# Loading the first block in two parts, alternating transposes and products on TensorE, and holding the first stores behind chunk 19

## Chip, cores and metric

The kernel runs on one core of one Trainium2 chip. The metric is the device time of one execution in microseconds (us). A core's span in the trace is from its first to its last instruction; it is about 1.5 us shorter than the time.

## The reference, cut to what matters

```python
# x: (16, 2048, 256) f32, so 32768 rows of 1 KB; W: (256, 256); A: (256, 16); B: (16, 256)
W_adapted = W + scale * (lora_A @ lora_B)
W_norm = np.sqrt(np.sum(W_adapted ** 2, axis=0, keepdims=True) + 1e-8)
W_final = W_adapted / W_norm * m
y = x.reshape(-1, 256) @ W_final          # 33.55 MB in, 33.55 MB out
```

## The kernel before

Eight blocks of 4096 rows (4 MB) go through five buffers. SyncE issues the loads, ScalarE the stores, each on its own DMA queue. The first five loads are issued at once; load b waits for store b - 5, which empties its buffer. A block has eight chunks of 512 rows; two chunks are a pair. A pair goes through four engines: GpSimd (POOL) casts it to bf16 into `xb`, TensorE (PE) turns it (eight transposes into `xt_ps`), VectorE (DVE) copies that to `xt`, TensorE multiplies by `w_final` into `y_ps` (16 matmuls), and ScalarE (ACT) copies the result into the block's own buffer, from where it is stored.

```python
parts = [(b * CH, CH) for b in range(NBLK - 1)]              # first chunk, chunks
parts += [(NCH - CH, CH // 2), (NCH - CH // 2, CH // 2)]     # last block in halves
...
for n in range(len(parts)):                                  # loads, on SyncE
    b = parts[n][0] // CH
    if b >= XBUFS and parts[n][0] % CH == 0:
        nc.sync.wait_ge(sem(f"store{b - XBUFS}"), 16)
    load_x(n)
...
for p in range(NPR):                                         # casts, on GpSimd
    if p == 0 or part_of[2 * p - 1] != part_of[2 * p]:
        nc.gpsimd.wait_ge(sem(f"load{part_of[2 * p]}"), 16)
    if p >= NXB:
        nc.gpsimd.wait_ge(sem("turned"), p - NXB + 1)
    nc.gpsimd.tensor_copy(out=xb_bufs[p % NXB][:], in_=...)
...
for g in range(NCH):                                         # results and stores, on ScalarE
    nc.scalar.wait_ge(sem("product"), g + 1)
    nc.scalar.copy(out=x_bufs[b % XBUFS][:, c * J : (c + 1) * J, :], in_=y_ps[g % 2][:])
    n = part_of[g]
    if g == NCH - 1 or part_of[g + 1] != n:
        store_y(n)                                           # after a drain
...
nc.tensor.wait_ge(dv, 8)                                     # w_final is ready
...
turned(0)
with nc.Fori(0, NPR // 2, 1, engines=[PE], head_slot={PE: 128}):
    turned(1)
    product(0)
    product(1)
    turned(0)
```

## Time and profile before

| | before |
|---|---|
| time, median of 4 runs | 163.69 us (163.48 to 163.89) |
| span of the profiled execution | 163.2 us |
| bytes, mean rate over the span | 67.41 MB, 413 GB/s |
| busiest compute engine | PE, 65% |

No compute engine is above 65%, and the DMA engines are full in every slice but the first and the last. So I took the bytes to be the bound (e9 below tests it); a change can then win only where the DMA queues are idle or slow. The prediction shows these rows. One more view: the start in order of time (start us, duration us, engine, line, operation, output and inputs, shapes, count, idle time before).

```profile
11.59 0.76 DVE L192 TENSOR_TENSOR wam<-wa,m_all 128x256 f32<-128x256 f32 x2
12.27 1.75 DVE L195 RECIPROCAL rnorm<-norm 128x256 f32<-128x256 f32 x1
13.83 3.92 POOL L165 CAST xb<-x_sb 128x2048 bf16<-128x2048 f32 x2 [12.15 <-DMA x_sb<-in_x_dram]
14.05 3.98 DVE L198 TENSOR_TENSOR w_final<-wam,rnorm 128x256 bf16<-128x256 f32 x2
```

The two multiplications of `wam` take 0.76 us, the two of `w_final`, with inputs of the same shape, 3.98, beside two casts.

### The profile page before, as it was taken

The page shows a single profiled execution, that of the slowest core. Times are in us where ns is not written, and L with a number is a line of the kernel's source. Part 1 is how long each engine was busy: PE and PEld are TensorE (multiplying, and loading weights), DVE is VectorE, ACT ScalarE, POOL GpSimd, SP SyncE. Part 2 cuts the span into 40 slices and gives each one's busy share as a digit, 9 for nine tenths or more (in the row PEclk, how much of TensorE's full clock was granted, in tenths as well). Part 3 has the DMA queues.
Part 4 walks back from the last instruction along what each step waited for, and adds up shares of the span by engine and source line. Part 5 has one row for each costly group of instructions (what it writes and reads, how often), then busy time and mean ns, then how long its engine had stood idle before and what let it go on. Part 6 is the DMA issues. An engine that isn't in the chain of part 4 may idle for free. (4 is left out here: it accounts for less than half of the span.)

```text
span 163.2 us, 1988 instructions
## 1 busy us (share of the span) xinstructions
PE 105.3 (65%) x786; PEld 85.2 (52%) x786; DVE 47.2 (29%) x44; ACT 63.8 (39%) x67; POOL 62.5 (38%) x39
## 2 busy tenths in 40 slices
PE   1270599789789897898981998619988820892000
PEld 0130577677577775776760867418676610771000
DVE  0429452350532514405230325005051400330000
ACT  3010027548366384473754053900738440062000
POOL 1006381753935738268004940069209003900000
PEclk9999999999999999999998589985899996599755
DMA  5998998998999999999999999999999999998991
GB/s 201 402 498 386 426 474 385 482 418 265 466 426 426 442 410 466 426 394 482 418 426 442 420 426 458 402 458 410 446 414 454 414 446 422 450 442 377 442 430 60
DMA packets 2915, 67.41 MB, mean 413 GB/s; under 512 B 465, under 2 KB 482, under 8 KB 610
## 3 DMA queue, kind: packets, MB, share of 16 engines
q1 hardware_dynamic: 1440, 33.82, 49.0%
q10 hardware_dynamic: 1474, 33.59, 47.8%
q14 instruction: 1, 0.01, 0.0%
HBM read 33.85 MB, written 33.55 MB: 413 GB/s over the span
## 5 line engine op out<-in xcount | busy, mean ns | idle before, releaser
L219 ACT COPY x_sb<-y_ps 128x1024 f32<-128x1024 f32 x64 | 61.9, 1014 | 75.8 <-PE y_ps L281 75.8
L165 POOL CAST xb<-x_sb 128x2048 bf16<-128x2048 f32 x32 | 60.0, 1902 | 79.3 <-DMA x_sb<-in_x_dram 56.0
L281 PE MATMUL y_ps<-w_final,xt 128*128 128x256 bf16 x512 | 64.6, 280 | 12.8 <-PEq L256 12.8
L202 DVE COPY xt<-xt_ps 128x1024 f32<-128x1024 f32 x32 | 38.2, 1221 | 88.1 <-PE xt_ps L267 88.0
L281 PEld LDWEIGHTS y_ps<-w_final,xt 128*128 128x128 bf16 x512 | 48.4, 100 | 28.2 <-issue 19.8
L267 PE MATMUL xt_ps<-identity,xb 128*128 128x128 f32 x264 | 39.1, 309 | 23.1 <-PEq L256 23.1
L267 PEld LDWEIGHTS xt_ps<-identity,xb 128*128 128x128 f32 x264 | 34.9, 161 | 25.8 <-issue 25.6
L198 DVE TENSOR_TENSOR w_final<-wam,rnorm 128x256 bf16<-128x256 f32 x2 | 4.0, 2028 | 0.0
L244 PE MATMUL y_ps<-sq,ones 128*128 128x256 f32 x4 | 2.1, 674 | 1.6 <-DVE sq L187 1.6
L233 PE MATMUL y_ps<-identity,a_nat 128*16 128x128 f32 x2 | 0.6, 397 | 3.6 <-DMA a_nat<-in_lora_A_dram 3.6
L212 ACT ACTIVATE norm<-y_ps,eps_col 128x256 f32<-128x256 f32 x1 | 0.5, 473 | 6.1 <-PE y_ps L244 6.1
L244 PEld LDWEIGHTS y_ps<-sq,ones 128*128 128x128 f32 x4 | 1.2, 323 | 2.3 <-DVE sq L187 2.1
L210 ACT ACT_TABLE_LOAD x1 | 1.3, 1283 | 2.4 <-issue 2.4
L233 PEld LDWEIGHTS y_ps<-identity,a_nat 128*16 128x16 f32 x2 | 0.1, 90 | 3.6 <-issue 3.6
L171 POOL MEMSET xb<- 128x2048 bf16 x1 | 1.8, 1805 | 0.3 <-PE xt_ps L267 0.3
L195 DVE RECIPROCAL rnorm<-norm 128x256 f32<-128x256 f32 x1 | 1.7, 1745 | 0.0
L237 PE MATMUL y_ps<-b_bf,aT 16*128 16x256 bf16 x2 | 0.6, 404 | 1.5 <-DVE aT L180 1.5
L189 DVE COPY m_all<-y_ps 128x256 f32<-128x256 f32 x1 | 0.4, 425 | 3.3 <-PE y_ps L249 3.3
L178 DVE CAST b_bf<-b_nat 16x256 bf16<-16x256 f32 x1 | 0.3, 281 | 3.8 <-DMA b_nat<-in_lora_B_dram 3.8
L249 PE MATMUL y_ps<-m_row,ones 1*128 1x256 f32 x2 | 1.2, 710 | 0.0
L237 PEld LDWEIGHTS y_ps<-b_bf,aT 16*128 16x128 bf16 x2 | 0.1, 106 | 1.9 <-DVE aT L180 1.9
L183 DVE SCALAR_TENSOR_TENSOR wa<-y_ps,w_nat 128x512 f32<-128x512 f32 x1 | 0.7, 692 | 0.8 <-PE y_ps L237 0.8
(13 smaller groups left out, 3.7 us busy)
## 6 DMA issues: line engine op xcount, KB each, us to landing
x_sb<-in_x_dram SPq DMA_DIRECT2D x7, 4096.0 KB, 27.1
out_dram<-x_sb ACTq DMA_DIRECT2D x7, 4096.0 KB, 37.2
x_sb<-in_x_dram SPq DMA_DIRECT2D x2, 2048.0 KB, 29.6
out_dram<-x_sb ACTq DMA_DIRECT2D x2, 2048.0 KB, 20.2
w_nat<-in_W_dram SPq DMA_DIRECT2D x1, 256.0 KB, 2.9
a_nat<-in_lora_A_dram ACTq DMA_DIRECT2D x1, 16.0 KB, 2.6
b_nat<-in_lora_B_dram ACTq DMA_DIRECT2D x1, 16.0 KB, 3.6
m_row<-in_m_dram ACTq DMA_DIRECT2D x1, 1.0 KB
```

What stands on the lines that cost most here:

```text
L165: nc.gpsimd.tensor_copy(out=xb_bufs[p % NXB][:], in_=x_bufs[b % XBUFS][:, 2 * c * J : 2 * (c + 1) * J, :],).then_inc(sem("rounded"), 1)
L171: nc.gpsimd.memset(xb_bufs[NPR % NXB][:], 0.0).then_inc(sem("rounded"), 1)
L183: nc.vector.scalar_tensor_tensor(out=wa[:], in0=ab_ps, scalar=float(scale), in1=w_nat[:], op0=ALU.mult, op1=ALU.add).then_inc(dv, 1)
L195: nc.vector.reciprocal(out=rnorm[:], in_=norm[:]).then_inc(dv, 1)
L198: i = nc.vector.tensor_mul(out=w_final[:, t], in0=wam[:, t], in1=rnorm[:])
L202: nc.vector.tensor_copy(out=xt_bufs[p % NXT][:].rearrange("p r t -> p (r t)").bitcast(FP32), in_=xt_ps[p % 2][:],).then_inc(sem("copied"), 1)
L210: nc.scalar.activation(out=warm[:], in_=eps_col[:], func=AF.Sqrt)
L219: nc.scalar.copy(out=x_bufs[b % XBUFS][:, c * J : (c + 1) * J, :], in_=y_ps[g % 2][:]).then_inc(sem("room"), 1)
L244: i = nc.tensor.matmul(n2_ps, ones[:], sq[:, t, :], start=(t == 0), stop=(t == KC - 1))
L249: nc.tensor.matmul(mb_ps, ones[0:1, :], m_row[:], start=True, stop=True).then_inc(pe, 1)
L267: i = nc.tensor.transpose(xt_ps[p % 2][:, j * P : (j + 1) * P], xb_bufs[p % NXB][:, j, :].bitcast(FP32), identity[:],)
L281: i = nc.tensor.matmul(y_ps[h][:, j, :], xt_bufs[p % NXT][:, r : r + P, t], w_final[:, t, :], start=(t == 0 and (j % (J // 2)) == 0), stop ...
```

## The change

Its intent: start TensorE earlier (the first pair needs only 1 MB, not 4), run it without gaps, and use the time so won to keep the stores back until the five free loads are nearly in, so that reads run alone first. Twelve tiny loads behind the last load mark in the trace when each of the DMA engines has done its loads. In the code, `turned(k)` is the eight transposes of the pair in buffer k and `product(k)` its 16 matmuls. The first cast also waits until VectorE has the squares of the weights (`dve`, 4). The diff, cut to its core (declarations, the DRAM layout of block 0 and the renaming of `parts` are left out):

```diff
+    HOLD = 19
+    MARKS = [1, 2, 3, 4, 5, 6, 8, 10, 12, 14, 15, 16]
-    parts = [(b * CH, CH) for b in range(NBLK - 1)]
-    parts += [(NCH - CH, CH // 2), (NCH - CH // 2, CH // 2)]
+    loads = [(0, 2), (2, CH - 2)] + [(b * CH, CH) for b in range(1, NBLK - 1)]
+    loads += [(NCH - CH, CH // 2), (NCH - CH // 2, CH // 2)]
+    stores = [(b * CH, CH) for b in range(NBLK - 1)]
+    stores += [(NCH - CH, CH // 2), (NCH - CH // 2, CH // 2)]
+    issue = [max(g0 + cnt - 1, HOLD + n) for n, (g0, cnt) in enumerate(stores)]
 ...
+    for q, n in enumerate(MARKS):
+        nc.sync.dma_start(
+            out=marks[0:n, q, 0 : 2 + n], in_=lora_B[0:n, 0 : 2 + n]
+        ).then_inc(sem("marks"), 16)
+    nc.sync.wait_ge(sem("marks"), 16 * len(MARKS))
 ...
+        if p == 0:
+            nc.gpsimd.wait_ge(sem("dve"), 4)
 ...
-        if g == NCH - 1 or part_of[g + 1] != n:
-            ...
-            store_y(n)
+        for n in range(len(stores)):
+            if issue[n] == g:
+                ...
+                store_y(n)
 ...
-    nc.tensor.wait_ge(dv, 8)
-    nc.tensor.sem_inc(sem("room"), 2)
     turned(0)
+    nc.tensor.wait_ge(dv, 8)
+    nc.tensor.sem_inc(sem("room"), 2)
     with nc.Fori(0, NPR // 2, 1, engines=[PE], head_slot={PE: 128}):
         turned(1)
         product(0)
+        turned(0)
         product(1)
-        turned(0)
```

More of the change, by code (lines that the diff above doesn't have):

```diff
@@ L85 @@
     m_all = sb("m_all", [P, OUT], FP32)
+    marks = sb("marks", [16, len(MARKS), 18], FP32)
     w_final = sb("w_final", [P, KC, OUT], BF16)
@@ L103, in sem @@
         return sems[name]
-    parts = [(b * CH, CH) for b in range(NBLK - 1)]
-    parts += [(NCH - CH, CH // 2), (NCH - CH // 2, CH // 2)]
-    part_of = {}
-    for n, (g0, cnt) in enumerate(parts):
-        for g in range(g0, g0 + cnt):
-            part_of[g] = n
+    loads = [(0, 2), (2, CH - 2)] + [(b * CH, CH) for b in range(1, NBLK - 1)]
+    loads += [(NCH - CH, CH // 2), (NCH - CH // 2, CH // 2)]
+    load_of = {g: n for n, (g0, cnt) in enumerate(loads) for g in range(g0, g0 + cnt)}
+    stores = [(b * CH, CH) for b in range(NBLK - 1)]
+    stores += [(NCH - CH, CH // 2), (NCH - CH // 2, CH // 2)]
+    issue = [max(g0 + cnt - 1, HOLD + n) for n, (g0, cnt) in enumerate(stores)]
     def in_sbuf(g0, cnt):
@@ L119, in in_dram @@
     def in_dram(dram, g0, cnt):
+        if g0 + cnt <= CH:
+            block = dram[0:BLK].rearrange("(p j) k -> p j k", p=P)
+            return block[:, g0 * J : (g0 + cnt) * J, :]
         return dram[g0 * J * P : (g0 + cnt) * J * P].rearrange("(p j) k -> p j k", p=P)
@@ L123, in load_x @@
         nc.sync.dma_start(
-            out=in_sbuf(*parts[n]), in_=in_dram(x_flat, *parts[n])
+            out=in_sbuf(*loads[n]), in_=in_dram(x_flat, *loads[n])
         ).then_inc(sem(f"load{n}"), 16)
@@ L128, in store_y @@
         nc.scalar.dma_start(
-            out=in_dram(out_flat, *parts[n]), in_=in_sbuf(*parts[n])
+            out=in_dram(out_flat, *stores[n]), in_=in_sbuf(*stores[n])
         ).then_inc(sem(f"store{n}"), 16)
@@ L140 @@
     nc.scalar.dma_start(out=m_row[:], in_=m[None, :]).then_inc(sem("load_m"), 16)
-    for n in range(len(parts)):
-        b = parts[n][0] // CH
-        if b >= XBUFS and parts[n][0] % CH == 0:
+    for n in range(len(loads)):
+        b = loads[n][0] // CH
+        if b >= XBUFS and loads[n][0] % CH == 0:
             nc.sync.wait_ge(sem(f"store{b - XBUFS}"), 16)
         load_x(n)
+    for q, n in enumerate(MARKS):
[3 more added lines that the diff above has]
+    nc.sync.wait_ge(sem("marks"), 16 * len(MARKS))
     nc.gpsimd.memset(zeros[:], 0.0).then_inc(sem("pool"), 1)
@@ L160 @@
         b, c = divmod(p, PRB)
-        if p == 0 or part_of[2 * p - 1] != part_of[2 * p]:
-            nc.gpsimd.wait_ge(sem(f"load{part_of[2 * p]}"), 16)
+        if p == 0 or load_of[2 * p - 1] != load_of[2 * p]:
+            nc.gpsimd.wait_ge(sem(f"load{load_of[2 * p]}"), 16)
+        if p == 0:
+            nc.gpsimd.wait_ge(sem("dve"), 4)
         if p >= NXB:
@@ L221 @@
         ).then_inc(sem("room"), 1)
-        n = part_of[g]
-        if g == NCH - 1 or part_of[g + 1] != n:
-            nc.scalar.drain().then_inc(sem("done"), 1)
-            nc.scalar.wait_ge(sem("done"), n + 1)
-            store_y(n)
+        for n in range(len(stores)):
+            if issue[n] == g:
+                nc.scalar.drain().then_inc(sem("done"), 1)
+                nc.scalar.wait_ge(sem("done"), n + 1)
+                store_y(n)
     pe = sem("pe")
```

## The prediction

> **What bounds the kernel now.** I read the span and the slice rows of the page first, then its queue rows, then a table of busy time by stretches of my own choosing, and last ScalarE in order of time. The first lines say how much was moved and that it was moved without a pause:
>
> ```profile
> span 163.2 us, 1988 instructions
> PE 105.3 (65%) x786; PEld 85.2 (52%) x786; DVE 47.2 (29%) x44; ACT 63.8 (39%) x67; POOL 62.5 (38%) x39
> ...
> DMA  5998998998999999999999999999999999998991
> ...
> DMA packets 2915, 67.41 MB, mean 413 GB/s; under 512 B 465, under 2 KB 482, under 8 KB 610
> ## 3 DMA queue, kind: packets, MB, share of 16 engines
> q1 hardware_dynamic: 1440, 33.82, 49.0%
> q10 hardware_dynamic: 1474, 33.59, 47.8%
> ```
>
> No compute engine passes 65%. The DMA engines are full in every slice but the first and the last; q1 carries the loads and q10 the stores. The table by stretches shows where the rate is not at its best (columns: stretch, its length, busy us of PE, PEld, DVE, ACT, POOL, clock, DMA share, GB/s; bytes are counted where a packet starts):
>
> ```profile
> 36.00:40.00 4.00, 3.68 (x34) 3.00 (x33) 0.63 (x1) 2.83 (x3) 2.04 (x2) 1.00 1.12 344
> 40.00:136.00 96.00, 73.21 (x576) 60.02 (x574) 28.55 (x24) 47.48 (x50) 41.09 (x22) 0.93 1.00 433
> 136.00:156.00 20.00, 8.33 (x56) 7.06 (x56) 2.45 (x2) 3.85 (x4) 5.54 (x3) 0.76 0.98 423
> 156.00:160.00 4.00, 0.00 (x0) 0.00 (x0) 0.00 (x0) 0.00 (x0) 0.00 (x0) 0.50 0.90 385
> 160.00:163.20 3.20, 0.00 (x0) 0.00 (x0) 0.00 (x0) 0.00 (x0) 0.00 (x0) 0.50 0.05 20
> ```
>
> With the bytes of each packet spread over its duration (my own sum over the packet records), the rate is 432 GB/s from 4 to 36 us, when there are only loads, 432 from 40 to 136, when loads and stores mix, and 432 from 136 to 156, when there are only stores. A 32 KB packet takes 1.213 us in both queues. So a mix of reads and writes costs no rate here. The one hole is 36 to 40 us at 299 GB/s. The first store is issued at 34.5, and from 36.1 on two load packets on each DMA engine take up to 2.9 us; each engine loses about 1.2 us, once.
>
> The end of a store shows another loss. Of the 16 completions of the last store, 15 come between 159.8 and 160.7 us, one at 163.2. One DMA engine lags 2.4 us. It has no lag when the loads alone end at 33.2; its store packets take some 50 ns longer than the 1.213 us from 47.7 to 150.4 us.
>
> This gives a ledger of the span: 2.75 us until packets flow, 67.41 MB at 432 GB/s = 156.0, hole 1.2, lag 2.4, last receipt 0.5. The sum is 162.9 against 163.2. Compute has no term in it. The chain of waits agrees: it stops at 145 us and holds 2% of the span, because from 148 us only stores run.
>
> **What the Trainium skill says.** "DMA: Bandwidth & Descriptors", section "Where 436 GB/s comes from", gives 435 GB/s as the ceiling of the 16 ports and says that HBM, at about 358, binds for transfers between HBM and SBUF. The trace agrees with the first (432) and not with the second. The same page, "Issuing engines are not separate DMA queues", says that transfers from several issuing engines share the same 16 DMA engines: 4 MB loads land 9.70 us apart alone (13.8, 23.5, 33.2) and 19.4 apart in the mix (48.8, 68.1). "SBUF — State Buffer", "Who interferes with whom", says that a VectorE instruction with two SBUF inputs contends with a GpSimd instruction that reads SBUF, and that the second to issue is blocked. The trace agrees: each half of w_final takes 2.03 us beside two casts, each half of wam, with the same inputs, 0.38 without one.
>
> **The change part by part.**
>
> *Block 0 in two loads.* No bytes are added. A 16 KB packet takes 0.611 us, half of a 32 KB one, so cutting 32 KB rows into 8 and 24 KB costs nothing that I can size. The first 1 MB should land near 6 us; the rest still lands at 13.8.
>
> *First turn early, w_final.* The first cast waits for the squares, done at 7.82, and runs 7.9 to 9.8, where VectorE is idle until 11.13. TensorE ends its preamble at 11.1 and turns pair 0 there. The second cast still waits for 13.8, and the third may follow at once, since pair 0 has been turned; so two casts still lie beside reciprocal and w_final, and w_final still ends at 18.0. What is saved is one turn at the slow start: 16 took 3.65 us, so 8 take about 1.8. The first product starts near 20.1 instead of 21.82.
>
> *By turns.* Before, one round of two pairs looks like this on ScalarE:
>
> ```profile
> 30.26 1.93 ACT L219 COPY x_sb<-y_ps 128x1024 f32<-128x1024 f32 x2 [2.45 <-PE y_ps L281]
> 32.49 1.93 ACT L219 COPY x_sb<-y_ps 128x1024 f32<-128x1024 f32 x2 [0.30 <-PE y_ps L281]
> 34.52 0.37 ACTq L128 DMA_DIRECT2D out_dram<-x_sb  x1
> 36.87 1.93 ACT L219 COPY x_sb<-y_ps 128x1024 f32<-128x1024 f32 x2 [2.46 <-PE y_ps L281]
> ```
>
> From 30.26 to 36.87 is 6.61 us for two pairs, 3.31 each. On TensorE that is 16 turns in 1.91, a gap of 0.69 (VectorE has only just begun to copy), 1.91 for a product, a gap of 0.32 (ScalarE has not given y_ps back) and 1.95. By turns, the copy of a pair runs beside the product of the pair before, and ScalarE's copies run beside the next turn, so both gaps go: 0.95 + 1.95 = 2.9 us per pair. POOL at 1.87 and ScalarE at 2.0 per pair fit in that. This saves 0.4 us per pair of compute, 13 us in 32 pairs, all of it beside full DMA queues: worth nothing by itself.
>
> *Stores held.* Product 0 ends near 20.1 + 2.7 = 22.8, product 9 at 22.8 + 9 x 2.9 = 48.9, chunk 19 is copied at 50.0, and store 0 is issued there, not at 34.5; store 1 at 52, store 2 near 56. Until then the loads run alone: block 4 lands at 13.8 + 4 x 9.70 = 52.6. A store starts to act 1.5 us after its issue (34.5 to 36.1), so at 51.5, some 0.6 us before the last load packets end at 52.1. The hole of 1.2 us moves there; as the loads run out in it, it may show as idle engines instead of slow packets. Then stores 0 and 1 run alone. Store 0 needs 9.7 us from about 53.3, lands near 63.8, and only then is load 5 issued (before: at 60.6). From 65.5 the two queues share. Store 1 has 3.1 MB left, 14.4 us in the mix, and load 5 lands near 85 (before 87.7), load 6 near 105 (107.4), the last half of load 7 near 124 (137.2). After that only stores run, some 15.7 MB = 36.3 us: 160, plus lag and receipt, 163. Since load 7 lands earlier by 13 us, and the product is faster, the last store is issued near 134, with about 26 us of stores ahead. The tail stays bound by DMA.
>
> *Marks.* Twelve loads of 12 to 1,152 bytes, issued behind load 7. A packet of 128 bytes takes 13 ns and a completion 9, so the DMA engine that serves all twelve spends about 0.3 us on them (an estimate from these two). If that is the lagging one, the end moves by 0.3.
>
> **Sum.** Bytes and rate: 0. Start: 0. Hole: 0, or up to +2 if chunk 19 comes later than 50.6. Restart of the loads after an empty queue near 65: 0, or a second hole of 1.2, taken at one in four, +0.3. Marks +0.1. Lag: the mix shrinks from about 100 us to 60, but the number of store packets in the slow time hardly changes, so 0 to -0.7. I choose +0.1 us: 163.8 us.
>
> **The rivals.** *Reads alone, then writes alone, are more efficient.* For it: the lag is nil at 33.2 us and grows during the mix, and the hole opens when stores start. If all the lag went, 2.4 us would be won: 161.3. Against it: 432 GB/s in all three kinds of stretch, and the long store packets go on from 137 to 150 us with no load about. *The queue runs dry between the last free load and the first store.* For it: the margin above is half a microsecond, and before, the first store packet starts 5.1 us after the issue. If those 5.1 us are pure latency, the engines idle from 52.1 to 55.1, 3.0 us in place of 1.2; each microsecond by which chunk 19 is late adds one. That gives 165.5 to 167. Against it: in those 5.1 us the load packets themselves are slow, so it looks more like a stall than like latency. *The faster, earlier compute shortens the kernel*: at 13 us of saved product time this would be 150 us. Against it: nothing waits for compute at the end; the last store waits 15.0 us from issue to landing, of which its own 2 MB need 4.9.
>
> **Range and chances.** Two percent are 3.3 us. A gain of 3.3 is more than lag and tail receipt together, so it would take two losses that vanish at once: 4%. A loss of 3.3 us needs the dry queue at its worst: 6%. The range is 161.8 (most of the lag won) to 166.2 (a dry queue of some 2.5 us).
>
> **What would show it.** Right: store 0 issued at 49 to 51 us; about 2.9 us per pair before; a stretch of reads alone at 432 GB/s to 52, one of stores alone to 65; last load landed near 124; the same mean GB/s, with the losses near 52 instead of 36; span 162 to 165. Wrong: a slice near 52 with the DMA share under a half (dry queue), or all 16 completions of the last store within a microsecond (the lag belongs to the mix), or a last store issued after 150 us.

## The result, and the profile after

| | before | after |
|---|---|---|
| time, median of 4 runs | 163.69 us | 163.74 us (163.58 to 163.99) |
| ratio of fast runs | | 1.0005, 95% interval 0.9986 to 1.0024 |
| span of the profiled execution | 163.2 us | 162.2 us |
| store 0 issued | 34.5 us | 45.5 us |
| last load landed | 137.2 us | 136.5 us |
| last store issued | 148.2 us | 149.8 us |

A ratio here and below is the mean time of one kernel's fast runs over that of the other's of the same rounds, so it is not quite the ratio of the medians quoted. Executions over 1.5% slower than the fastest of the same kernel are left out of the means.

The time is the same. The profiled span is 1.0 us shorter, but that is not the change. The profiled execution of before took 164.71 us, longer than any of its four timed runs; in 11 later runs of that kernel, beside the first experiments, the span was 161.9 to 162.7 us. The trace of before is an unusually slow execution, so differences under a microsecond between the two traces mean nothing.

The page of the changed kernel:

```profile
span 162.2 us, 2003 instructions
PE 100.9 (62%) x786; PEld 87.8 (54%) x786; DVE 44.9 (28%) x44; ACT 64.2 (40%) x67; POOL 62.5 (39%) x39
...
DMA  4999999999998999999999999999999999999993
...
DMA packets 3251, 67.42 MB, mean 416 GB/s; under 512 B 673, under 2 KB 690, under 8 KB 818
## 3 DMA queue, kind: packets, MB, share of 16 engines
q1 hardware_dynamic: 1776, 33.82, 49.2%
q10 hardware_dynamic: 1474, 33.59, 48.2%
```

The bytes are the same, and the DMA row is as full. The table by stretches (columns as in the prediction's) shows the losses moved:

```profile
48.00:52.00 4.00, 3.90 (x37) 3.36 (x35) 2.24 (x2) 3.06 (x4) 3.01 (x2) 1.00 1.06 369
52.00:65.00 13.00, 11.61 (x107) 10.62 (x105) 4.90 (x4) 8.65 (x10) 8.06 (x5) 1.00 1.00 431
65.00:136.00 71.00, 37.06 (x283) 32.28 (x281) 14.70 (x12) 23.86 (x25) 18.77 (x10) 0.76 1.00 430
136.00:156.00 20.00, 10.01 (x72) 8.64 (x72) 2.45 (x2) 5.88 (x6) 5.54 (x3) 0.76 1.00 426
156.00:160.00 4.00, 0.00 (x0) 0.00 (x0) 0.00 (x0) 0.00 (x0) 0.00 (x0) 0.50 0.88 377
```

The slow stretch is now at 48 to 52 us, where store 0 joins the loads, instead of 36 to 40. With the bytes spread over the packets' durations, the rate is 432 to 434 GB/s from 6 to 44 us (reads alone), 432 from 56 to 64 (stores alone: the free loads are in, and load 5 waits for store 0, which lands at 63.7), and about 432 in the mix after that. What falls short of 432 GB/s adds up to 0.90 us between 40 and 65 us, against 1.17 us between 5 and 40 us before.

The compute did get faster. ScalarE in order of time:

```profile
27.70 1.93 ACT L237 COPY x_sb<-y_ps 128x1024 f32<-128x1024 f32 x2 [0.72 <-PE y_ps L295]
30.32 1.93 ACT L237 COPY x_sb<-y_ps 128x1024 f32<-128x1024 f32 x2 [0.69 <-PE y_ps L295]
...
45.46 0.37 ACTq L136 DMA_DIRECT2D out_dram<-x_sb  x1
...
149.83 0.34 ACTq L136 DMA_DIRECT2D out_dram<-x_sb  x1
```

A pair takes 30.32 - 27.70 = 2.62 us instead of 3.31. The start also differs:

```profile
7.26 1.89 POOL L183 CAST xb<-x_sb 128x2048 bf16<-128x2048 f32 x1 [5.58 <-DVE sq L205]
...
13.35 0.76 DVE L216 TENSOR_TENSOR w_final<-wam,rnorm 128x256 bf16<-128x256 f32 x2
13.97 3.73 POOL L183 CAST xb<-x_sb 128x2048 bf16<-128x2048 f32 x2 [4.83 <-DMA x_sb<-in_x_dram]
...
17.74 2.91 PE L295 MATMUL y_ps<-w_final,xt 128*128 128x256 bf16 x16
```

Here `w_final` began before the casts and was not held up: 0.76 us instead of 3.98. The first product starts at 17.74 us, not 21.82.

### The profile page after: what moved, and what is told of

It reads as the page before. It is cut to its first block, busy times and chain, and to the rows that moved or that the text cites. A ratio compares the mean times of both kernels' runs of the same rounds, so it can differ in the third digit from the quotient of the medians.

```text
span 162.2 us, 2003 instructions
## 1 busy us (share of the span) xinstructions
PE 100.9 (62%) x786; PEld 87.8 (54%) x786; DVE 44.9 (28%) x44; ACT 64.2 (40%) x67; POOL 62.5 (39%) x39
## 5 line engine op out<-in xcount | busy, mean ns | idle before, releaser
L183 POOL CAST xb<-x_sb 128x2048 bf16<-128x2048 f32 x32 | 60.0, 1893 | 78.6 <-DMA x_sb<-in_x_dram 63.5
L295 PE MATMUL y_ps<-w_final,xt 128*128 128x256 bf16 x512 | 66.8, 288 | 0.1
L220 DVE COPY xt<-xt_ps 128x1024 f32<-128x1024 f32 x32 | 39.2, 1225 | 92.3 <-PE xt_ps L281 92.3
L281 PEld LDWEIGHTS xt_ps<-identity,xb 128*128 128x128 f32 x264 | 33.8, 156 | 44.4 <-issue 44.0
L295 PEld LDWEIGHTS y_ps<-w_final,xt 128*128 128x128 bf16 x512 | 53.0, 104 | 8.4 <-issue 0.4
L267 PEld LDWEIGHTS y_ps<-m_row,ones 1*128 1x128 f32 x2 | 0.5, 308 | 0.7 <-issue 0.7
```

The lines of the kernel that those rows point to most:

```text
L183: nc.gpsimd.tensor_copy(out=xb_bufs[p % NXB][:], in_=x_bufs[b % XBUFS][:, 2 * c * J : 2 * (c + 1) * J, :],).then_inc(sem("rounded"), 1)
L220: nc.vector.tensor_copy(out=xt_bufs[p % NXT][:].rearrange("p r t -> p (r t)").bitcast(FP32), in_=xt_ps[p % 2][:],).then_inc(sem("copied"), 1)
L267: nc.tensor.matmul(mb_ps, ones[0:1, :], m_row[:], start=True, stop=True).then_inc(pe, 1)
L281: i = nc.tensor.transpose(xt_ps[p % 2][:, j * P : (j + 1) * P], xb_bufs[p % NXB][:, j, :].bitcast(FP32), identity[:],)
L295: i = nc.tensor.matmul(y_ps[h][:, j, :], xt_bufs[p % NXT][:, r : r + P, t], w_final[:, t, :], start=(t == 0 and (j % (J // 2)) == 0), stop ...
```

## The experiments

Ten kernels ran. Theory: the bytes at 432 GB/s set the time, and none of the change's parts touches them. Its main rival: a part wins what another loses. "Lost" below is the time by which the rate, with the bytes spread over the packets' durations, falls short of 432 GB/s in a stretch; a recount from the packet records gave the same within 0.2 us.

### e1: without the marks

```diff
-    for q, n in enumerate(MARKS):
-        nc.sync.dma_start(...).then_inc(sem("marks"), 16)
-    nc.sync.wait_ge(sem("marks"), 16 * len(MARKS))
```

> The changed kernel without its twelve marks. Theory (the DMA engines bound both kernels and the marks are a few hundred nanoseconds of work on one of them): 163.6 us, 0 to 0.3 us below the changed kernel. Rival (a small transfer stalls its DMA engine until its receipt is back, so the marks cost a microsecond that the rest of the change had won): 162.6 us or less.

163.61 us, ratio to before 0.9995 (0.9972 to 1.0018). The marks cost nothing that shows.

### e2: without the hold

```diff
-    HOLD = 19
+    HOLD = 0
```

> The changed kernel with its stores issued as soon as a block is done; block 0 in two loads and the turns stay. Theory (faster compute and held stores are both worth nothing, since the rate is 432 GB/s whatever the mix): 163.7 us, store 0 issued near 30 us, the hole of about 1 us right after it. Rival (the hold wins what the rest loses, or the reverse): over 0.5 us away from 163.7.

163.97 us, ratio 1.0011 (0.9990 to 1.0032), with one of six runs slow at 170.09, which is left out. Store 0 was issued at 29.5 us, and 1.0 us was lost right after it, at 31 to 37, as expected. Not expected was the end. Without the hold the stores take their share of the rate earlier, so the loads come later: the last landed at 142.1 us instead of 136.5, and the last two stores were issued at 150.1 and 155.4. Store 6 had largely drained by 150.7, so the queues had little to do:

```profile
148.00:152.00 4.00, 4.00 (x38) 3.68 (x36) 1.23 (x1) 3.12 (x4) 0.00 (x0) 0.97 0.83 349
```

The new order on TensorE has a share in this. `turned(0)` of the next pair now stands before `product(1)` of a block's last pair, and it needs the next load. So the last pair of the first half of block 7, whose load had landed at 127.3, was copied only after the second half had landed at 142.1 (ScalarE, the line with 11.95 us of waiting):

```profile
133.97 1.93 ACT L237 COPY x_sb<-y_ps 128x1024 f32<-128x1024 f32 x2 [0.69 <-PE y_ps L295]
147.85 2.17 ACT L237 COPY x_sb<-y_ps 128x1024 f32<-128x1024 f32 x2 [11.95 <-PE y_ps L295]
150.12 0.34 ACTq L136 DMA_DIRECT2D out_dram<-x_sb  x1
```

The store of that half was issued 22.8 us after its load landed, here and in the changed kernel (121.8 to 144.6), against 10.6 us before (122.3 to 132.9). From 65 to 160 us 1.3 us were lost. Yet the time hardly moved, because the other loss shrank: the 16 completions of the last store fell within 0.7 us, against 2.6 in the changed kernel. The completions of store 6, before the dry stretch, were 2.3 us apart, those of the next store 1.2: it looks as if the lagging DMA engines caught up while the others had nothing to do. So the hold is worth nothing in time here; it moves spare time to the tail.

### e3: store 0 held until chunk 23

```diff
-    HOLD = 19
+    HOLD = 23
```

> The changed kernel with store 0 held until chunk 23, issued near 50.9 us, where the free loads end at about 52.1. Theory (the hole at the first store is a stall of about 1 us, which begins 1.5 us after the issue): no packets for about 1.5 us in all near 53, so 163.7 to 164.5 us. Rival (the 4.5 us from the first issue to the first store packet are pure latency, hidden only while loads remain): engines idle from 52.1 to 55.4, some 3.3 us in place of 0.9, so 166 us.

165.31 us, ratio 1.0094 (1.0074 to 1.0115): between the two expectations, and the trace refutes both. Store 0 was issued at 51.0 us, and its first packet started at 51.87, 0.9 us later, so the 4.5 us of the changed kernel are no fixed latency; only 0.5 us was lost between 40 and 65. Nor is the hole a stall that belongs to the first store, since 1.2 us were now lost later, in two stretches:

```profile
50.00:54.00 4.00, 4.00 (x39) 3.62 (x36) 1.90 (x2) 2.22 (x3) 2.48 (x3) 1.00 1.00 377
66.00:70.00 4.00, 2.97 (x28) 2.51 (x25) 1.22 (x1) 3.31 (x4) 0.00 (x0) 1.00 1.03 377
76.00:80.00 4.00, 0.00 (x0) 0.00 (x0) 0.00 (x0) 0.00 (x0) 0.00 (x0) 0.50 0.91 336
```

At 66 to 70 us load 5 joins the stores, and it is the store packets that are slow. The second stretch, near the end of store 1, has no join to explain it. The runs do not settle the mechanism. What they show is that a queue which joins a full one often costs about a microsecond, and not always: in the changed kernel load 5 joined the stores at 65 us at no cost.

### e4: the hold alone, on the kernel before

```diff
+    issue = [max(g0 + cnt - 1, 19 + n) for n, (g0, cnt) in enumerate(parts)]
-        if g == NCH - 1 or part_of[g + 1] != n:
+        for n in range(len(parts)):
+            if issue[n] == g:
```

> The kernel before with the held stores alone (no early first turn, TensorE in its old order, block 0 in one load, no marks). At 3.31 us per pair chunk 19 is ready at 54.4 us, after the free loads end at 52.1. Theory: the DMA engines idle from 52.1 to about 56.5 or 57.5, 4.4 to 5.4 us, less the 1.2 us of the hole that goes: 166.9 to 168.2 us. Rival (reads alone and then writes alone pay back): 165 us or less.

166.82 us, ratio 1.0182 (1.0158 to 1.0207), just below what was expected: slower, though not surely by 2%. With the old pace store 0 was issued at 54.7 us, after the free loads had landed at 52.6:

```profile
52.00:56.00 4.00, 3.31 (x31) 2.86 (x30) 1.56 (x2) 2.27 (x3) 1.47 (x1) 1.00 0.31 131
...
68.00:72.00 4.00, 3.05 (x27) 2.40 (x25) 2.36 (x2) 1.55 (x3) 3.60 (x2) 1.00 0.90 270
```

The queues were dry for most of 52 to 56 us; 3.8 us were lost there, and 1.6 more when load 5 joined and at 82. This is the one part that was seen to cost time by itself (the early first turn and the new order ran only together, in e2). With the faster compute the cost is gone, since store 0 comes at 45.5 us.

### e5: no compute

The casts, turns, copies and products are taken out, and the blocks are stored as they were loaded. Its output is wrong, which doesn't matter for the time.

```diff
-    for g in range(NCH): ...            # results and stores
+    nc.scalar.wait_ge(sem(f"load{load_of[4 * CH - 1]}"), 16)
+    for n, (g0, cnt) in enumerate(stores):
+        for k in sorted({load_of[g] for g in range(g0, g0 + cnt)}):
+            nc.scalar.wait_ge(sem(f"load{k}"), 16)
+        store_y(n)
```

> The changed kernel without its stages of casts, turns, copies and products; the blocks go out as they came in (wrong on purpose), store 0 behind the load of block 3, which lands at 42.8 us, so near the issue of 45.5. Theory (67.4 MB at 432 GB/s set the time and 100 us of TensorE work set none of it): 162.5 to 163.8 us. If the lag of one DMA engine comes from the compute beside it, the 16 completions of the last store fall within 0.8 us and the time is at the low end. Rival (compute has a share in the end): under 161.5 us.

162.35 us, ratio 0.9925 (0.9891 to 0.9959), a little below what was expected. The page:

```profile
span 161.1 us, 141 instructions
PE 4.4 (3%) x10; PEld 1.9 (1%) x10; DVE 5.8 (4%) x12; ACT 2.0 (1%) x3; POOL 0.7 (0%) x6
...
DMA  4999999999999999999999999999999999999996
```

With 96 us of TensorE work gone, 1.3 us are won. About 1.0 of them lies in the span and shows at the end of the last store; the rest lies outside the span (time less span is 1.3 us here, about 1.5 before). The 16 completions of the last store fall within 1.2 us (3.3 in the trace of before, 2.6 in the changed kernel). Store packets that take 20 to 150 ns too long are 4, against 40 and 38. In this trace no DMA engine lags as before. That the lag comes from the compute is likely, but not shown: this is one trace, another of the four runs took 163.38 us (span 162.1), as long as with compute, and the stores were issued at other times too (the first four at 43.0 to 44.4 us, the last at 135.9). Nor does the number of long packets settle it: e2 has about 145 of them with completions 0.7 us apart, e4 about 90 with 2.0.

### e6: the last block in one load

```diff
-    loads += [(NCH - CH, CH // 2), (NCH - CH // 2, CH // 2)]
+    loads += [(NCH - CH, CH)]
```

(The DRAM side of the last block follows the block's layout, as it does for block 0.)

> The changed kernel with the last block loaded in one transfer of 32 KB rows instead of two of 16 KB rows. Theory (the two queues take turns packet by packet, so 16 KB packets against 32 KB packets get one third of the rate, 140 against 290 GB/s in the trace): load 7 gets 216 GB/s and lands near 127 us instead of 136.5, the last store is issued near 141 instead of 149.8, and the time stays at 163.7, within 0.3, since the last store only waits longer. Rival (the last load is on the path to the end): 161 to 163 us.

Load 7 landed at 126.5 us instead of 136.5. While it ran, both queues moved packets of 32 KB in nearly equal numbers (114 and 110 ended from 109 to 126 us, 220 and 212 GB/s). In the changed kernel, from 109 to 128 us, 168 load packets of 16 KB ended beside 166 store packets of 32 KB, 145 beside 286 GB/s. The queues take turns packet by packet, and the smaller packet gets the smaller share. The time was 164.03 us, ratio 1.0038 (1.0010 to 1.0066): ten microseconds earlier on the last load gained nothing. It was even a little slower; one run of the six, at 165.44, carries part of that, the others are 163.79 to 164.27. Its trace has a stretch at 76 to 80 us in which about 0.5 us was lost, but e1's has it too and is not slower.

### e7: a small store early

```diff
+    nc.scalar.dma_start(
+        out=in_dram(out_flat, *stores[-1])[:, 0, 0:P], in_=ones[:]
+    ).then_inc(sem("early"), 16)
```

(The last store also waits for it, so that it is overwritten; that line is left out.)

> The changed kernel with a store of 64 KB near 1.5 us, overwritten later. Rival (the hole of 0.9 us at 48 us is the price of the kernel's first writes, paid once): the hole goes from there, and 162.8 us if nothing takes its place near 3 us. Theory now (it comes when a queue joins one that is full, as at 66 to 70 us with loads joining stores in the two kernels with late stores): the hole stays at 47 to 50 us, 163.7 us.

163.92 us, ratio 1.0019 (1.0005 to 1.0033). The slow packets at 47 to 49 us stayed, with 0.64 us lost, so the hole is not the price of the kernel's first write. The early store itself took long: issued at 2.4 us, its 64 KB landed at 14.2, just after the second load of block 0. Its 128 packets of 512 bytes show why: they start in eight rounds of 16, from 6.6 to 13.6 us, one round every 0.93 us, which is one load packet of 24 KB (0.91 us) and one of 512 bytes (0.03). Packet by packet again, and the small packet gets almost nothing.

### e8 and e9: fewer bytes

Their outputs are wrong, which doesn't matter for the times.

```diff
-            out=in_sbuf(*loads[n]), in_=in_dram(x_flat, *loads[n])
+            out=in_sbuf(*loads[n])[0:k], in_=in_dram(x_flat, *loads[n])[0:k]         # e8, k = 16 in block 6
+            out=in_sbuf(*loads[n])[:, 0:k], in_=in_dram(x_flat, *loads[n])[:, 0:k]   # e9, k = 4 rows in block 6
```

> The changed kernel that reads 16 of 128 partitions of block 6, so 3.67 MB less (wrong on purpose). Theory: 3.67 MB at 432 GB/s are 8.5 us, so 155.2 us, within 0.7. Rival (something beside bytes bounds the later half, such as the chain of load, compute and store through five buffers): 157.5 us or more.

158.34 us: 5.3 us won, not 8.5, and on the rival's side of its line. But the experiment was badly built, as its table by stretches shows:

```profile
86.00:92.00 6.00, 2.40 (x12) 2.18 (x13) 0.42 (x1) 0.00 (x0) 4.12 (x3) 0.50 1.00 235
```

The load into 16 neighbouring partitions ran at 32 KB per 3.1 to 3.8 us and DMA engine, and slowed the whole core. The Trainium skill, "SBUF — State Buffer", section "Door 1: The DMA port swizzle", says that partitions 0 to 15 reach four of the 16 ports, and gives 104 GB/s for them, measured with 1 MiB; the 0.52 MB here took 5.0 us (86.5 to 91.5), 106 GB/s. So the same bytes were taken away across all partitions:

> The run with fewer bytes again, mended: e8 read 16 neighbouring partitions, and its rate fell to 166 to 280 GB/s from 86 to 92 us (2.7 us lost of the 8.5 expected). Here block 6 is read on all 128 partitions, 4 of 32 rows each: the same 3.67 MB less (wrong on purpose). Theory (bytes at 432 GB/s): 155.2 us, within 0.7, without a stretch under 400 GB/s near 86 to 92. Rival (the chain through the five buffers bounds the later half): over 157 us again.

155.56 us, ratio 0.9502 (0.9479 to 0.9525): 8.2 us won of 8.5. The mended stretch:

```profile
86.00:92.00 6.00, 2.72 (x13) 2.44 (x14) 0.74 (x1) 0.00 (x0) 4.44 (x3) 0.50 0.94 403
```

Bytes set the time, at 3.67 MB per 8.2 us.

### e10: no hold, no marks, the last block in one load

```diff
-    HOLD = 19
+    HOLD = 0
-    loads += [(NCH - CH, CH // 2), (NCH - CH // 2, CH // 2)]
+    loads += [(NCH - CH, CH)]
```

> An attempt at a version better than both: no hold, no marks, the last block in one load, the rest of the changed kernel. In e2 (no hold) the last load landed at 142 us and the queues ran dry before the last two stores, near 150; with 32 KB packets the last load lands about 7 us earlier, so that hole (1.1 us) goes. Theory: the lag of one DMA engine, which the dry stretch had hidden, comes back, so 163.3 to 163.9 us, no better than before. Rival (the dry stretch was a pure loss): 162.6 us.

163.76 us, ratio 0.9987 (0.9962 to 1.0011). The dry stretch of e2 was gone (nothing lost from 65 to 158 us), and the lag was back: the 16 completions of the last store spread over 2.9 us. Neither kernel was beaten. By chance this run also shows how little the start matters. Here lora_B landed late, and the casts won against `w_final` again:

```profile
13.74 3.92 POOL L178 CAST xb<-x_sb 128x2048 bf16<-128x2048 f32 x2 [3.86 <-DMA x_sb<-in_x_dram]
14.08 3.85 DVE L211 TENSOR_TENSOR w_final<-wam,rnorm 128x256 bf16<-128x256 f32 x2
```

Store 0 was issued at 32.4 us, 2.9 later than in e2, and the time was no worse.

## Why the prediction was right

The time, 163.8 forecast and 163.74 measured, rests on one step: the change removes no bytes, and the ledger has no term for compute. e9 shows the slope in bytes, e5 that all the compute together is worth 1.3 us. Within that, several steps were off without moving the sum, and of the signs that I named for being right, four did not come: store 0 at 49 to 51 us, 2.9 us per pair, reads alone to 52, the last load near 124. No sign of being wrong came, one only just not (the last store at 149.8, with the line at 150). The agreement to 0.1 us is luck, since the four runs alone differ by 0.4 us.

- **Restart of the loads, hole, marks.** Small terms, as forecast: 0.90 us at the first store, nothing at 65 us, nothing for the marks. (A slip in a sum: 53.3 + 9.7 is 63.0, or 63.5 with the receipt, not 63.8; store 0 landed at 63.7.) But the account of the hole, a stall that begins 1.5 us after the first store's issue, fell with e3, where the first store started cleanly and the loss came later. What makes the hole stays open.
- **w_final.** I had it end at 18.0 us, held by two casts. It ended at 14.1. lora_B landed at about 4.3 us instead of 5.0, the chain behind it ran 0.7 us earlier, and `w_final` came ahead of the cast instead of 0.2 us behind it. The split of block 0 may have done this, which I did not see: in the two traces with block 0 in one load (before, e4) one of the 16 completions of lora_B came 0.8 to 1.0 us after the other 15, about as long as a 32 KB packet takes, and with 8 KB packets none came more than 0.3 us after the rest. It is not shown, and in e10 all 16 were late and the casts won again. A margin of a few tenths decided 3 us, and I took the side that one trace showed as a property.
- **Pair and chunk 19.** 2.9 us per pair was the sum of two busy times (0.95 + 1.95). In the trace the groups overlap at their ends (a turn of 1.04 us starts at 120.16, the next product at 121.03); back to back, a pair takes 2.62. The prediction's own list showed the overlap: its five items add up to 6.78 us, not to the 6.61 measured. With the earlier start, store 0 came at 45.5 us and not at 50.0. That was luck: I had reckoned half a microsecond of margin to a dry queue. The margin was in fact wider: at 51.0 (e3) the first store packet came before the last load packets were done, at 54.7 (e4) the queue was dry.
- **Last load near 124 us.** It landed at 136.5. The step took half the rate for each queue; the last block's 16 KB packets get a third. e6 removes that and gives 126.5. With it fell the last store's issue (134 forecast, 149.8 measured) and most of the spare time that I had put at the end: the last store waited 12.4 us from issue to landing, not 28. The figures were at hand, since 2 MB of load 7 had taken 14.9 us in the mix before (122.3 to 137.2), where half the rate would have been 9.7. I also missed what the new order does at a block's end (see e2): a block's last pair waits for the next load, and one such pair stood ahead of the last store, which was issued 13.3 us after the last load landed, against 11.0 before.
- **Lag.** Forecast as 0 to -0.7 us. The traces show 2.5 us before and 1.3 after between the last two completions of the last store, but the trace of before is a slow execution, and the other kernels with compute give 0.4 (e4) to 2.2 (e8). No effect of the change on it can be claimed.
- **The rivals.** "Reads alone, then writes alone, are more efficient" is refuted: reads alone, stores alone and the mix all run at 430 to 434 GB/s, and e3, with the longest time of reads alone at full load, is slower by 0.9%. The dry queue was avoided, and is real in e4. Compute at the end is hidden, with less to spare than I thought: in e2 it came to the surface for about a microsecond, by the new order and the later loads together.

So the expected gain went nowhere: the compute time saved, 0.7 us in each of 32 pairs, lay beside full DMA queues, and the held stores only changed the order of the same bytes.

## What to carry to other kernels

When the DMA row is full from end to end and each kind of stretch runs at the same rate, list the losses (start, holes, lag, last receipt) before weighing a reordering: here they were about 7 us of 163 in the trace of before, and only they could be won. When you reorder an engine's work, look at the block's end too: what is put first may wait for a load that what comes second does not need. Look at the spread of the runs before reading a difference between two traces, because one profiled execution can be a microsecond off. When two queues share the DMA engines, compare their packet sizes before you halve the rate between them.

## What the Trainium skill lacked or had wrong

- "DMA: Bandwidth & Descriptors", "Queues, rings and completion order", says that a DMA engine goes round its queues packet by packet. It does not say that the rate is then shared by packet size: 168 packets of 16 KB against 166 of 32 KB, 145 against 286 GB/s.
- The same page, "Where 436 GB/s comes from", has HBM bind at about 358 GB/s between HBM and SBUF; here one core ran at 430 to 434 GB/s in reads, in writes and in the mix. A note in the section "Measured" of that page gives about 358 for the case that both cores of an HBM domain stream; the passage itself does not say so.
- No page that I found has the cost of a queue that joins a full one: 0.6 to 1.2 us lost at the first store, and 4.5 to 5.1 us from issue to first packet, against 0.9 us when the loads were done or in their last packets.
- None that I found has store packets that take longer beside compute (the first page, "Latency and other measured facts", has DMA engines 7/15 as usually slower, and guesses at descriptors written by software; both queues here are hardware ones): in before and the changed kernel about 40 packets by some 50 ns, with last completions 2.6 to 3.3 us apart, against 4 packets and 1.2 us in the one trace without compute. The cause is open.
